# Key sums in one product of 384 rows, token factors spread by transfers, last columns in halves, and an opening by three queues, in a hybrid attention layer

## The chip, the core and the metric

The kernel runs on one core of a Trainium2 chip. The metric is the device time of one execution in microseconds. TensorE is called PE below (its weight loads PEld), VectorE DVE, ScalarE ACT, GpSimd POOL, and SyncE SP. SP, ACT and POOL can issue transfers; what each has issued stands in a queue of its own, and the 16 DMA engines serve all queues.

## What is computed

One layer of an encoder for 256 tokens (two blocks of 128) of width 2048, all in float32. It has two groups of eight heads of 128, then a feed-forward part with a causal convolution:

```python
h  = rms_norm(x)
p  = h @ w_in                      # q, k, v of both groups and the forget gates
a  = forgetting_attention(...)     # softmax with a bias of summed log forget gates
b  = stick_breaking_attention(...) # strictly causal, weights from suffix sums
x  = x + concat(rms_norm(a), rms_norm(b)) @ w_out
h  = rms_norm(x)
u  = causal_conv3(h @ w_up) + conv_b
x  = x + (silu(gate_of(u)) * value_of(u)) @ w_down        # d_ff = 5632

# stick breaking, one head
z             = q @ k.T * scale
log_beta      = log_sigmoid(z)
log_one_minus = where(mask, log_beta - z, 0)
suffix        = reversed_cumsum(log_one_minus, over keys) - log_one_minus
weights       = where(mask, exp(log_beta + suffix), 0)
out           = weights @ v
```

## The kernel before

**Products in three parts.** Weights arrive as float32 (`w_raw`, by SP's queue). ACT casts them to float32r (`w_hi`, L197), DVE subtracts that from the original (`w_lo`, L198), and activations are split in the same way. Each product is then the sum of three: high by high, low by high, high by low. Token-major results have 512 columns a product (`in_three`, L219), feature-major ones take 512 columns for both parts of hT by `w_hi` (L246) and 256 columns by `w_lo` (L253). A piece of weights is 1 MB in most stages.

**Order.** The opening and the feed-forward part have an order written out by hand for PE, DVE, ACT and SP (`manual_schedule`). Between them a scheduler orders the instructions of each engine. The feed-forward part is a list of steps: step n issues its loads six steps ahead, splits weights two steps ahead, and what follows a step (`follow`) runs in the steps after it. Within one engine, instructions run in their order, so a waiting instruction holds all behind it.

**Opening.** `opening` (from L353) computes the first 512 columns, the queries of the first four heads, while x is still arriving. `columns` (L125) turns the rows of the first norm's gains (`prow`) into a column `ga`, with the identity from the constants `cs`; `transposed_split` transposes x (L135), scales it by `ga` into the high part of hT on ACT (L140) and makes the low part on DVE (L143). `split_w` casts and splits weights (L374, L377), `multiply` (L386) accumulates. `keep_busy` (L349) sends products of a cleared tile `zeros` through PE while the first data are on their way. The weights of the first piece come as two blocks of 256 KB by ACT's queue; x, `cs` and the rest by SP's.

**Token factors.** The factor of RMSNorm for each token is not applied to x but to the results. `token_factors` computes it as a column per block (`rstd`, L114). Where results have tokens in partitions, it is used as it is. Where tokens run along the free axis (feature-major results), each partition needs all 256 factors in a row: `in_every_partition` multiplies a matrix of ones by two diagonal matrices `dg` (L163) on PE (L170) and copies the result from PSUM to a tile R (L171). R1 is used for the queries and keys of the stick-breaking heads (`R1q` at L558 is R1 times the scale), R2 in the feed-forward part (`convolved`, L695), from step 1 on.

**First heads.** `fox_rows` takes the query rows of four heads, forms the factor of each head's norm on DVE and ACT (L108 to L114), multiplies (`raw`, L313), and `to_heads` transposes on PE (L294).

**Stick breaking.** `sb_head` has the logits of a head in one PSUM tile `ps` of three blocks of 128 columns: `ps[:, 0]` for keys 0 to 127 by queries 0 to 127, `ps[:, 1]` for the same keys by queries 128 to 255, `ps[:, 2]` for keys and queries 128 to 255. `z0` is the first two, `z1` the third, `zz` all. The key sums are added to it by products with a triangle of -1 (`ntri[:, :P]`) and a square of -1 (`ntri[:, P:]`), once for each part of the split sums `sps` (L595 to L597).

**End.** `down_plain` computes the last rows of the down projection: for each 512 columns two pieces of weights of four row blocks. For the last 512 columns the second piece does token block 0 first and then token block 1; DVE adds each result to x (L792) and SP stores it (L794), for block 1 in two parts of 256 columns.

**POOL** issues the transfers of `c_rows` (L492, a row for each head written to DRAM) and `minus_c` (L493, the same rows read into all partitions), and some of the weights in the feed-forward part (L815).

Of the kernel before, what the change touches and what calls it, by code (L numbers as in the profile page):

```python
# [14 lines left out]
P = 128  # L15
# [26 lines left out]
def hybrid_layer(  # L42
# [123 lines left out]
    def in_every_partition(dg, n, pool):  # L166
        R = pool.tile([P, S], F32, name=f"R{n}")
        pr = psb.tile([P, S], F32, name="pr", tag="t")
        for t in range(NT):
            nc.tensor.matmul(pr[:, t * P : (t + 1) * P], ones, dg[t], start=t == 0, stop=t == NT - 1)  # L170
        dve.tensor_copy(R, pr)  # L171
        return R


# [99 lines left out]
    with ExitStack() as actx:  # L274
# [78 lines left out]
        def opening():  # L353

            acc = psa.tile([P, NT, 512], F32, name="acc", tag="acc")
            pairs = [[(0, 1), (1, 1)]] + [[(0, 2)]] * 7
            raws, parts = [], []

            def load_w(c, queue=nc.sync, which=(0, 1)):
                if c == len(raws):  # L360
                    raws.append(wraw.tile([P, 2048], F32, name="w_raw", tag="w_raw"))
                for i, n in pairs[c][which[0] : which[-1] + 1]:
                    queue.dma_start(
                        raws[c][:, i * 512 : (i + n) * 512].rearrange("p (a b) -> p a b", a=n),
                        rows_of(wi, 2 * c + i, n, 0, 512),
                    )
# [13 lines left out]

            def multiply(c, i, n, high):
                hi, lo = (p[:, i : i + n] for p in parts[c])
                order = [(j, l, hi) for j in range(n) for l in range(2)] if high else [(j, 0, lo) for j in range(n)]
                for m, (j, l, r) in enumerate(order):
                    for t in range(NT):
                        nc.tensor.matmul(  # L386
                            acc[:, t, :], of_half(hT[:, 2 * c + i + j], l, t), r[:, j, :],
                            start=high and c == i == m == 0, stop=not high and c == 7 and m == n - 1,
                        )
# [12 lines left out]
            columns(ga, prow[:KT, :], KT)  # L402
            keep_busy(0)
            split_w(0)
            keep_busy(6)

            def behind(c):
                transposed_split(2 * c + 2, ga)
                split_w(c + 1)

            for c in range(8):
                if 0 < c < 7:
                    behind(c)
                for i, n in pairs[c]:
                    if i == 0:
                        if c:
                            sums_of_squares(ss1, c // 2, [c % 2])
                        if c < 5:
                            if c % 2:
                                load_x(8 + 4 * (c // 2), 4)  # L420
                            load_w(c + 3)
                    for high in (True, False):
                        multiply(c, i, n, high)
                        if c == i == 0 and high:
                            behind(0)
                            sums_of_squares(ss1, 0, [0])
            return acc
# [7 lines left out]
        rstd1, dg1 = token_factors(ss1, 1)  # L435

        columns(pcol, prow, 50)
        masksR = at.tile([P, 4 * P], F32R, name="masksR")
# [28 lines left out]

        c_of = at.tile([P, NT, NH], F32, name="c_of")
        minus_c = at.tile([P, NH, S], F32, name="minus_c")
        dram = actx.enter_context(tc.tile_pool(name="dram", bufs=1, space=bass.MemoryType.DRAM))  # L470
        c_rows = dram.tile([NH, S], F32, name="c_rows")

        def gates():
# [79 lines left out]


        B0 = 3 * WF + NH
        R1 = in_every_partition(dg1, 1, at)
        R1q = at.tile([P, S], F32, name="R1q")
        dve.tensor_scalar(R1q, R1, QSCALE, None, op0=ALU.mult)  # L558

# [10 lines left out]
        def sb_head(h, qT, kT, v):  # L570
# [21 lines left out]

            for i in range(2):
                s = sps[:, i, :]
                mm(z0, ntri[:, :P], s[:, : 2 * P], start=False, stop=False, skip_group_check=True)  # L595
                mm(ps[:, 1, :], ntri[:, P:], s[:, 2 * P :], start=False, stop=False, skip_group_check=True)
                mm(z1, ntri[:, :P], s[:, 2 * P :], start=False, stop=i == 1, skip_group_check=True)  # L597
# [68 lines left out]
    tokens = []  # L666

    def parameters():
        pc = psb.tile([P, 4, NC2], F32, name="pcc", tag="t")
# [117 lines left out]
        yield  # L787

    def added(c, ps, t, op=ALU.add, final=False, n=512):
        for i in range(0, 512, n):  # L790
            xs = xt[t][:, c + i : c + i + n]
            dve.tensor_tensor(xs, xs, ps[:, i : i + n], op=op)  # L792
            if final:
                nc.sync.dma_start(of[t * P : (t + 1) * P, c + i : c + i + n], xs)  # L794
        yield

    def down_in_seven(part, c0):
# [70 lines left out]
    def down_plain(part, c):  # L868

        n = (part.f_hi - part.f_lo) // 4  # L870
        cell = []

        def piece(kh):
            mem = {}

            ends = c == D - 512 and kh == n - 1

            def loads():
                mem["raw"] = load(rows_of(wd, part.f_lo + 4 * kh, 4, c, 512))

            def prepare():
                mem["parts"] = split(mem["raw"], 4, 512)

            def matmuls():
                if kh == 0 and c == D - 512:
                    cell.extend(psf.tile([P, 512], F32, name="bank_a", tag="a") for _ in range(NT))
                elif kh == 0:
                    acc = psa.tile([P, NT, 512], F32, name="acc", tag="acc")
                    cell.extend(acc[:, t, :] for t in range(NT))
                for ts in [[t] for t in range(NT)] if ends else [range(NT)]:  # L890
                    in_three(
                        [cell[t] for t in ts], mem["parts"], 4,
                        lambda i, p, t: of_half(part.pairs[2 * kh + i // 2][:, :, i % 2], p, ts[t]),
                        kh == 0, kh == n - 1,
                    )
# [41 lines left out]
    for n in range(-LOAD, len(steps) + 8):  # L937
# [4 lines left out]
        with tc.high_priority(offset=2 * AHEAD) if n < 0 else nullcontext():  # L942
# [62 lines left out]
```

## Time and profile before

| | |
|---|---|
| median of three runs | 1116.93 us (1116.54 to 1117.72) |
| profiled execution | 1115.63 us |
| its span | 1113.7 us |
| PE busy | 1106.9 us, 99% |
| DVE busy | 862.7 us, 77% |
| ACT busy | 692.7 us, 62% |
| POOL busy | 27.2 us, 2% |
| read from memory over the span | 207 GB/s |

The profile is of one execution. A row of the timeline gives start, length, engine, line of the kernel, operation, output and inputs, and in brackets how long the engine was idle before and what ended that. PEq, SPq and the like are instruction queues. The chain of waits is followed back from the last instruction: at each step to what released it, or to the instruction before it on its engine; its rows are start, length and what, so that the length of a product there is its pace and not its way through the array.

### The profile page before, as it was taken

How to read it: one execution, taken by the hardware profiler on the slowest of the kernel's cores; microseconds unless marked ns; L12 is line 12 of the kernel's file. 1: busy time of each engine (PE TensorE's matmuls, PEld its weight loads, DVE VectorE, ACT ScalarE, POOL GpSimd, SP SyncE). 2: the span in 40 equal slices, each digit the busy share in tenths (PEclk: the TensorE clock that was granted, in tenths of full speed). 3: DMA queues.
4: the chain of work that ended last, by engine and by line, in shares of the span. 5: the costliest groups of instructions: out<-in, count | busy, mean ns of one | idle time of the engine just before them, and what ended most of it. 6: DMA issues, size and time to landing. Idle time of an engine off the chain costs nothing.

```text
span 1113.7 us, 14715 instructions
## 1 busy us (share of the span) xinstructions
PE 1106.9 (99%) x5873; PEld 957.9 (86%) x5873; DVE 862.7 (77%) x906; ACT 692.7 (62%) x849; POOL 27.2 (2%) x27
## 2 busy tenths in 40 slices
PE   9999999999999999999999999999999999999998
PEld 7998888888888888888888888888888888888886
DVE  5745666657666677788899898989989899989973
ACT  6544545355565567666777767775777667776751
POOL 0000000000000000000000000000000000000000
PEclk9999999999999999999999999999999999999999
DMA  8676656564445486496869696788859697697941
GB/s 260 213 227 227 190 152 189 155 185 153 152 152 164 137 271 207 126 263 181 259 211 254 208 265 218 227 243 228 248 184 251 219 266 248 193 266 195 297 161 67
DMA packets 172479, 231.34 MB, mean 208 GB/s; under 512 B 4192, under 2 KB 118266, under 8 KB 172282
## 3 DMA queue, kind: packets, MB, share of 16 engines
q1 hardware_dynamic: 162378, 209.93, 58.3%
q0 software_dynamic: 9712, 19.93, 10.2%
q8 instruction: 46, 0.75, 0.3%
q10 hardware_dynamic: 320, 0.53, 0.2%
q14 instruction: 23, 0.19, 0.0%
HBM read 228.28 MB, written 2.11 MB: 207 GB/s over the span
## 4 chain that ended last, share of the span: by engine, by line
PE 98%; DVE 1%; DMA 0%; ACT 0%; issue 0%; SPq 0%; DVEq 0%; ACTq 0%
PE pu L246 33%; PE acc L219 24%; PE pu L253 18%; PE bank_a L219 10%; PE bank_b L219 4%; PE bank_c L219 2%; PE acc L386 2%; PE ps_x L135 1%; DVE w_lo L198 1%; DMA cs<-in_cst_dram 0%; PE ps_z L576 0%; PE ps_o L604 0%; PE ps_s L506 0%; PE ps_o L536 0%; PE ps_h L294 0%; PE ps_p L530 0%
## 5 line engine op out<-in xcount | busy, mean ns | idle before, releaser
L198 DVE TENSOR_TENSOR w_lo<-w_raw,w_hi 128x2048 fp32r<-128x2048 f32 (+2 forms) x200 | 440.1, 2204 | 161.9 <-ACT w_hi L197 156.0
L197 ACT CAST w_hi<-w_raw 128x2048 fp32r<-128x2048 f32 (+2 forms) x200 | 368.1, 1841 | 239.4 <-PE acc L219 91.2
L246 PE MATMUL pu<-hT,w_hi 128*128 128x512 f32 x1664 | 397.6, 391 | 0.0
L246 PEld LDWEIGHTS pu<-hT,w_hi 128*128 128x128 f32 x1664 | 310.1, 188 | 63.2
L253 PEld LDWEIGHTS pu<-hT,w_lo 128*128 128x128 f32 x1664 | 213.6, 191 | 8.2
L253 PE MATMUL pu<-hT,w_lo 128*128 128x256 f32 x1664 | 216.2, 283 | 0.0
L219 PE MATMUL acc<-w_hi,hT 128*128 128x512 f32 (+1 forms) x576 | 126.0, 370 | 0.0
L219 PEld LDWEIGHTS acc<-w_hi,hT 128*128 128x128 f32 x576 | 101.6, 188 | 14.3
L709 ACT ACTIVATE tap<-up,ccol 128x256 f32<-128x256 f32 x176 | 74.6, 495 | 0.0
L198 DVE TENSOR_TENSOR w_lo<-w_sum,w_hi 128x2048 fp32r<-128x2048 f32 (+1 forms) x30 | 62.2, 2073 | 13.4 <-ACT w_hi L197 10.6
L197 ACT CAST w_hi<-w_sum 128x2048 fp32r<-128x2048 f32 (+1 forms) x30 | 51.9, 1731 | 22.8 <-PE pu L246 22.8
L219 PE MATMUL acc<-w_lo,hT 128*128 128x512 f32 (+1 forms) x288 | 64.6, 366 | 0.0
L219 PEld LDWEIGHTS acc<-w_lo,hT 128*128 128x128 f32 x288 | 51.6, 188 | 7.5
L219 PE MATMUL acc<-w_hi,oT 128*128 128x512 f32 x192 | 46.3, 393 | 0.0
L219 PE MATMUL bank_a<-w_hi,g 128*128 128x512 f32 x176 | 44.2, 392 | 0.0
L219 PEld LDWEIGHTS acc<-w_hi,oT 128*128 128x128 f32 x192 | 35.4, 188 | 7.0
L219 PEld LDWEIGHTS bank_a<-w_hi,g 128*128 128x128 f32 x176 | 31.8, 189 | 5.7
L219 PE MATMUL bank_a<-w_hi,s 128*128 128x512 f32 x144 | 36.5, 393 | 0.0
L219 PE MATMUL bank_b<-w_hi,s 128*128 128x512 f32 x144 | 36.4, 392 | 0.0
L714 DVE TENSOR_TENSOR gate<-gate,tap 128x512 f32<-128x512 f32 x44 | 30.3, 688 | 2.3
L714 DVE TENSOR_TENSOR val<-val,tap 128x512 f32<-128x512 f32 x44 | 30.3, 688 | 2.3
L815 POOL DMA_DIRECT2D w_raw<-in_w_down_dram x10 | 12.7, 1270 | 779.6 <-DVE s L761 373.9
(176 smaller groups left out, 1052.1 us busy)
## 6 DMA issues: line engine op xcount, KB each, us to landing
w_raw<-in_w_up_dram SPq DMA_DIRECT2D x88, 1024.0 KB, 5.8
w_raw<-in_w_down_dram SPq DMA_DIRECT2D x40, 1024.0 KB, 5.3
w_raw<-in_w_in_dram SPq DMA_DIRECT2D x36, 1024.0 KB, 5.3
w_raw<-in_w_out_dram SPq DMA_DIRECT2D x16, 1024.0 KB, 5.2
w_raw<-in_w_in_dram SPq DMA_DIRECT2D x12, 688.0 KB, 4.2
w_raw<-in_w_down_dram POOLq DMA_DIRECT2D x8, 1024.0 KB, 12.0
w_sum<-in_w_down_dram POOLq DMA_DIRECT2D x8, 1024.0 KB, 9.0
w_raw<-in_w_down_dram SPq DMA_DIRECT2D x8, 512.0 KB, 4.0
```

Source lines behind the costliest of these rows:

```text
L135: nc.tensor.transpose(ps[:, j, t * P : (t + 1) * P], xt[t][:, (k + j) * P : (k + j + 1) * P], ident)
L197: act.copy(hi[:, :n], raw[:, :n])
L198: dve.tensor_tensor(lo[:, :n], raw[:, :n], f32(hi[:, :n]), op=ALU.subtract)
L219: nc.tensor.matmul(o, lhs(i, l, t), r[:, i, :], start=starts and j == 0, stop=stops and j == 3 * n - 1, skip_group_check=more,)
L246: nc.tensor.matmul(acc[:, j, :], hi[:, i, j * P : (j + 1) * P], hT[:, k].rearrange("p a b -> p (a b)"), start=k == 0, stop=False,)
L253: nc.tensor.matmul(acc[:, j, S:], lo[:, i, j * P : (j + 1) * P], hT[:, k, 0, :], start=False, stop=k == KT - 1,)
L386: nc.tensor.matmul(acc[:, t, :], of_half(hT[:, 2 * c + i + j], l, t), r[:, j, :], start=high and c == i == m == 0, stop=not high and c == ...
L709: act.activation(taps[w][:, j, :], u[:, j, w : w + S], AF.Copy, scale=ccol[:, w, f : f + 1])
L714: dve.tensor_tensor(a, a, tap, op=ALU.add)
L815: nc.gpsimd.dma_start(mem[into][:, : nk * 512].rearrange("p (a b) -> p a b", a=nk), src, accum_op=ALU.add)
```

## The change

Five edits, in the order of the kernel:

- `token_factors` makes no diagonal matrices. `in_every_partition` writes each block's column of factors to a row in DRAM by POOL (128 elements of 4 bytes a transfer), and reads both rows into all partitions by a third transfer, which waits for the two. For R2 it is called right after the factors, and not in step 1 of the feed-forward part.
- The opening: `cs` and the rows of gains go to POOL's queue; the first 256 columns of x come as one transfer for each token block, on SP and on ACT; the first block of weights follows on SP, the second on ACT. DVE clears `zeros` and makes the first `w_hi`. PE gets 16 and 5 products of `keep_busy`, before 17 and 6.
- `sb_head`: one product of all 384 columns with the triangle, and one of 128 with the square.
- `added` has one part at each call.
- `down_plain`: for the last 512 columns token block 1 is computed as two results of 256 columns in tiles of their own. In the first piece the three results take turns, in the second they come one after the other, and each is added and stored when it is done.

In the built kernel `R1q` moves on DVE from 155 us, among the softmax work of the first group, to the place between L108 and L111 of the first query heads. Moved lines of the same text are left out here:

```diff
-        dg = []
         for t in range(NT):
-            dg.append(small.tile([P, P], F32, name="dg", tag="dg", bufs=2))
-            dve.tensor_scalar(dg[t], ident, rstd[:, t : t + 1], None, op0=ALU.mult)
-        return rstd, dg
...
-    def in_every_partition(dg, n, pool):
-        R = pool.tile([P, S], F32, name=f"R{n}")
-        pr = psb.tile([P, S], F32, name="pr", tag="t")
-        for t in range(NT):
-            nc.tensor.matmul(pr[:, t * P : (t + 1) * P], ones, dg[t], start=t == 0, stop=t == NT - 1)
-        dve.tensor_copy(R, pr)
+    def in_every_partition(rstd, n, pool):
+        row = dram.tile([NT, P], F32, name=f"row{n}")
+        R = pool.tile([P, S], F32, name=f"R{n}")
+        for t in range(NT):
+            nc.gpsimd.dma_start(row[t : t + 1, :].rearrange("t p -> p t"), rstd[:, t : t + 1])
+        nc.gpsimd.dma_start(R, row.rearrange("t p -> (t p)").unsqueeze(0).to_broadcast([P, S]))
         return R
...
-        nc.gpsimd.memset(zeros, 0.0)
+        dve.memset(zeros, 0.0)
...
-                    act.copy(hi[:, cols], raws[c][:, cols])
                     if c == i == 0:
+                        dve.tensor_copy(hi[:, cols], raws[c][:, cols])
                         transposed_split(0, ga)
+                    else:
+                        act.copy(hi[:, cols], raws[c][:, cols])
...
-            load_x(0, 2)
-            nc.sync.dma_start(cs[:, :P], cst[:, :P])
-            load_w(0, nc.scalar, [0])
-            nc.scalar.dma_start(prow[:KT, :], attn_norm[0].rearrange("(n p) -> n p", p=P))
+            nc.gpsimd.dma_start(cs[:, :P], cst[:, :P])
+            nc.gpsimd.dma_start(prow[:KT, :], attn_norm[0].rearrange("(n p) -> n p", p=P))
+            for t, queue in enumerate((nc.sync, nc.scalar)):
+                queue.dma_start(xt[t][:, : 2 * P], xf[t * P : (t + 1) * P, : 2 * P])
+            load_w(0, nc.sync, [0])
             load_w(0, nc.scalar, [1])
...
-            keep_busy(17)
+            keep_busy(16)
             columns(ga, prow[:KT, :], KT)
-            keep_busy(0)
             split_w(0)
-            keep_busy(6)
+            keep_busy(5)
...
-                mm(z0, ntri[:, :P], s[:, : 2 * P], start=False, stop=False, skip_group_check=True)
-                mm(ps[:, 1, :], ntri[:, P:], s[:, 2 * P :], start=False, stop=False, skip_group_check=True)
-                mm(z1, ntri[:, :P], s[:, 2 * P :], start=False, stop=i == 1, skip_group_check=True)
+                mm(zz, ntri[:, :P], s, start=False, stop=False, skip_group_check=True)
+                mm(ps[:, 1, :], ntri[:, P:], s[:, 2 * P :], start=False, stop=i == 1, skip_group_check=True)
...
-    rstd2, dg2 = token_factors(ss2, 2)
+    rstd2 = token_factors(ss2, 2)
+    tokens = [in_every_partition(rstd2, 2, const)]
...
     def down_plain(part, c):
...
+        ends = c == D - 512
+        sizes = [(0, 0, 512), (1, 0, 256), (1, 256, 256)] if ends else [(t, 0, 512) for t in range(NT)]
+        cells = []
...
+            def product(some):
+                hi, lo = mem["parts"]
+                order = [(i, l, hi) for i in range(4) for l in range(2)] + [(i, 0, lo) for i in range(4)]
+                for j, (i, l, r) in enumerate(order):
+                    g = part.pairs[2 * kh + i // 2][:, :, i % 2]
+                    for (t, c0, cols), o in some:
+                        nc.tensor.matmul(
+                            o, of_half(g, l, t), r[:, i, c0 : c0 + cols],
+                            start=kh == 0 and j == 0, stop=kh == n - 1 and j == 11,
+                        )
...
+                both = list(zip(sizes, cells))
+                for some in [[b] for b in both] if ends and kh == n - 1 else [both]:
+                    product(some)
...
             def follow():
-                for t in range(NT):
-                    yield from added(c, cell[t], t, final=True, n=256 if ends and t else 512)
+                for (t, c0, cols), o in zip(sizes, cells):
+                    yield from added(c + c0, o, t, final=True, n=cols)
...
-            if n == 1:
-                tokens.append(in_every_partition(dg2, 2, const))
```

More of the change, by code (lines that the diff above doesn't have):

```diff
@@ L159, in token_factors @@
         rsqrt(rstd, ssum, 1.0 / D, NT)
-        dg = []
-        for t in range(NT):
-            dg.append(small.tile([P, P], F32, name="dg", tag="dg", bufs=2))
-            dve.tensor_scalar(dg[t], ident, rstd[:, t : t + 1], None, op0=ALU.mult)
-        return rstd, dg
-    def in_every_partition(dg, n, pool):
-        R = pool.tile([P, S], F32, name=f"R{n}")
-        pr = psb.tile([P, S], F32, name="pr", tag="t")
-        for t in range(NT):
-            nc.tensor.matmul(pr[:, t * P : (t + 1) * P], ones, dg[t], start=t == 0, stop=t == NT - 1)
-        dve.tensor_copy(R, pr)
+        return rstd
+    dram = ctx.enter_context(tc.tile_pool(name="dram", bufs=1, space=bass.MemoryType.DRAM))
+    def in_every_partition(rstd, n, pool):
+        row = dram.tile([NT, P], F32, name=f"row{n}")
+        R = pool.tile([P, S], F32, name=f"R{n}")
+        for t in range(NT):
+            nc.gpsimd.dma_start(row[t : t + 1, :].rearrange("t p -> p t"), rstd[:, t : t + 1])
+        nc.gpsimd.dma_start(R, row.rearrange("t p -> (t p)").unsqueeze(0).to_broadcast([P, S]))
         return R
@@ L434, in hybrid_layer @@
         load_parameters(masks)
[L435 removed]
+        rstd1 = token_factors(ss1, 1)
         columns(pcol, prow, 50)
@@ L789, in added @@
     def added(c, ps, t, op=ALU.add, final=False, n=512):
[L790 to L794, printed above, removed]
+        xs = xt[t][:, c : c + n]
+        dve.tensor_tensor(xs, xs, ps, op=op)
+        if final:
+            nc.sync.dma_start(of[t * P : (t + 1) * P, c : c + n], xs)
         yield
@@ L882, in prepare @@
                 mem["parts"] = split(mem["raw"], 4, 512)
+            def product(some):
[8 more added lines that the diff above has]
+                        )
             def matmuls():
-                if kh == 0 and c == D - 512:
-                    cell.extend(psf.tile([P, 512], F32, name="bank_a", tag="a") for _ in range(NT))
+                if kh == 0 and ends:
+                    for i, (_, _, cols) in enumerate(sizes):
+                        pool, tag = (psf, "a") if i < 2 else (psb, "t")
+                        cells.append(pool.tile([P, 512], F32, name="bank_a", tag=tag)[:, :cols])
                 elif kh == 0:
                     acc = psa.tile([P, NT, 512], F32, name="acc", tag="acc")
[L889 to L895, printed above, removed]
+                    cells.extend(acc[:, t, :] for t in range(NT))
+                both = list(zip(sizes, cells))
+                for some in [[b] for b in both] if ends and kh == n - 1 else [both]:
+                    product(some)
             def follow():
-                for t in range(NT):
-                    yield from added(c, cell[t], t, final=True, n=256 if ends and t else 512)
+                for (t, c0, cols), o in zip(sizes, cells):
+                    yield from added(c + c0, o, t, final=True, n=cols)
             new_step(loads, None, prepare, matmuls, follow if kh == n - 1 else None)
```

6 lines of the change are left out of this document (1 added, 5 removed).

## The prediction

> **What bounds the kernel now.** I read the page first, then the chain of waits stretch by stretch, then the timeline at the places that the change touches.
>
> ```profile
> PE 1106.9 (99%) x5873; PEld 957.9 (86%) x5873; DVE 862.7 (77%) x906; ACT 692.7 (62%) x849; POOL 27.2 (2%) x27
> PE 98%; DVE 1%; DMA 0%; ACT 0%; issue 0%; SPq 0%; DVEq 0%; ACTq 0%
> ```
>
> TensorE (PE) is busy for 99% of the span and is 98% of the chain. So an instruction taken from PE is worth its whole pace, wherever its operands are ready, and a wait that reaches PE costs its whole length. GpSimd (POOL) is free, and PE stands still only in the first microseconds, after the token factors, and at the end. The change touches these three places, and two products in the middle. The profiled execution took 1115.63 us, its span is 1113.7 and 1.9 us lie around it. The sum below is made on the span and carried to the median of the runs, 1116.93, which is 1.3 us above the profiled one.
>
> **The opening.** Chain of waits, then the timeline's row of the first real weight load:
>
> ```profile
> 1.23 4.08 DMA cs<-in_cst_dram
> ...
> 7.69 0.73 PE acc L386 x2
> ...
> 10.79 0.44 PE ps_x L135 x4
> ```
> ```profile
> 5.42 0.13 PEld L125 LDWEIGHTS pp<-cs,prow 16*128 16x128 f32 x1 [1.25 <-DMA prow<-in_attn_norm_dram]
> ```
>
> Everything hangs on the identity (`cs`, 64 KB) and the norm rows (`prow`, 8 KB), which arrive together at 5.3 to 5.4 us, `cs` behind the first x on SP, `prow` behind the first weights on ACT. The DMA issues of the opening give their sizes (KB each, us to landing):
>
> ```profile
> w_raw<-in_w_in_dram ACTq DMA_DIRECT2D x2, 256.0 KB, 5.0
> x<-in_x_dram SPq DMA_DIRECT2D x2, 256.0 KB, 5.1
> ```
>
> The change gives `cs` and `prow` to POOL's queue, puts half of the first x at the head of SP and half at the head of ACT, the first weights second on SP, and moves the first `w_hi` copy to DVE, which is idle there until hT comes. What can it bring? A look at the DMA engines:
>
> ```profile
> 5.00:10.00 5.00, 4.40 (x25) 3.31 (x26) 2.48 (x6) 2.81 (x7) 0.00 (x0) 1.00 1.00 362
> ```
>
> Between 5 and 10 us they are full (share 1.00, 362 GB/s), and the bytes needed by the transposes at 10.79 stay the same. So beyond about 0.9 us an earlier start would only wait there for x: an estimate, the size of PE's idle time in these 5 us (5.00 less 4.40) and half as much again. That bounds the gain. On the other side, POOL issues `cs` first and `prow` after it, 0.6 to 0.7 us each (rows below), while SP and ACT issue both first weight blocks. If `prow` has to stand behind these, it comes after 832 KB (x, `cs`, two blocks) instead of 584 KB (x, `cs`, `prow`, one block), 248 KB later, at 362 GB/s 0.7 us; a little of that is saved in front of it. So the bounds are -0.9 and +0.6; I take -0.3, between them and nearer to the gain, since `cs` and x themselves stand behind less in either order. Two idle products fewer and the cleared tile on DVE cost nothing: PE waits for data behind both.
>
> **Token factors, what goes.** Chain of waits at the two places where the factors are spread by PE:
>
> ```profile
> 151.30 0.44 PE pr L170 x4
> ```
> ```profile
> 414.86 0.45 PE pr L170 x4
> ```
>
> Both stand on the chain with PE full on either side, so removing them gives -0.89. The DVE work that goes (`dg`, the copy of R) is off the path.
>
> **Token factors, what comes.** Each time POOL issues two column writes of 128 single elements and a read that waits for both and spreads them. What such a round trip costs is seen at `c_rows`, the one that exists: POOL's timeline, the issues with their time to landing, and the DMA queues from 95.2 to 98 and from 98.5 to 101:
>
> ```profile
> 92.53 0.69 POOL L492 DMA_DIRECT2D c_rows<-mine  x1 [91.49 <-ACT mine L491]
> 94.61 0.59 POOL L493 DMA_DIRECT2D minus_c<-c_rows  x1 [1.39 <-DMA c_rows<-mine]
> ```
> ```profile
> w_raw<-in_w_in_dram SPq DMA_DIRECT2D x12, 688.0 KB, 4.2
> ...
> minus_c<-c_rows POOLq DMA_DIRECT2D x1, 1024.0 KB, 7.0
> ...
> c_rows<-mine POOLq DMA_DIRECT2D x1, 8.0 KB, 1.8
> ```
> ```profile
> q1 hardware_dynamic: 417, 0.85, 93.4%
> ```
> ```profile
> q0 software_dynamic: 130, 0.97, 92.0%
> ```
>
> With the engines idle a write took 1.8 us and its reader could be issued 2.08 us after it. But the read, issued by 95.2, moved nothing until 98: SP's queue (q1) had the engines to itself, and only then did POOL's (q0) run, with 92%. So a small transfer of POOL stands behind the loads that SP has already issued. That decides when R1 and R2 come.
>
> The order of the built kernel puts `R1q` (which needs R1) on DVE right after `rs_a` of the first query heads, far earlier than today's 155 us. Timeline of DVE, then two loads of SP:
>
> ```profile
> 35.96 0.16 DVE L114 TENSOR_TENSOR rstd<-rs_y,rs_u 128x2 f32<-128x2 f32 x1
> ```
> ```profile
> 42.47 0.24 DVE L108 TENSOR_SCALAR rs_a<-ss 128x4 f32<-128x4 f32 x2
> 43.14 0.26 DVE L111 TENSOR_TENSOR rs_u<-rs_a,rs_y 128x4 f32<-128x4 f32 x2 [0.44 <-ACT rs_y L110]
> ```
> ```profile
> 38.68 0.37 SPq L190 DMA_DIRECT2D w_raw<-in_w_in_dram  x1
> ```
> ```profile
> 42.58 0.37 SPq L190 DMA_DIRECT2D w_raw<-in_w_in_dram  x1
> ```
>
> The factor is ready at 36.12. Two issues of about 0.69 and 2.08 us from the second one's start give landed columns at about 39.0, a little more for 256 tiny elements beside a load: 39.7. The read is issued by 40.4 and stands behind the load of 38.68, which lands 4.2 us after its issue, at 42.9; 128 KB more, 43.4. `R1q` (an estimate of 0.3 us, less than a pass over 256 columns of PSUM) ends at 43.7, where today `rs_u` starts at 43.14. Behind it in DVE's queue stand `rs_u`, `r` and `raw`; PE's head transposes wait for `raw`, so PE loses what DVE loses: +0.6. From below it is 0 (R1 in time), from above it is the third rival.
>
> For R2 the view is the same, with more cover:
>
> ```profile
> 418.81 0.69 DVE L695 TENSOR_TENSOR up<-t,R 128x512 f32<-128x512 f32 x1
> ```
> ```profile
> 429.31 0.69 DVE L693 TENSOR_TENSOR t<-pu,t 128x512 f32<-128x512 f32 x1
> ```
> ```profile
> 437.76 3.82 PE L246 MATMUL pu<-hT,w_hi 128*128 128x512 f32 x16
> ```
>
> This factor is ready at about 411 (the product that spreads it today stands at 414.86). The round trip without loads takes some 5 us (0.69 and 2.08 for the columns, about 2 for the read); a load of 1 MB in front of a step costs 2.8 us (95.2 to 98 above). With one or two in front of each of the two steps R2 comes at 421 to 427, 3 to 8 us after DVE wants it at 418.81. Queued behind that wait on DVE are `ccol`, two `w_lo` and the next `t`; on ACT the taps, the next cast and SiLU. But PE needs that `t` (it frees the PSUM bank) only at 437.76, and today it is done at 430.0. The cover is 7.8 us and some idle time on DVE and ACT more. So I put 0; beyond some 10 us of wait PE pays all the rest.
>
> **Key sums.** Chain of waits, one head of eight:
>
> ```profile
> 274.81 0.12 PE ps_z L595
> 274.93 0.06 PE ps_z L596
> 274.99 0.12 PE ps_z L597
> 275.11 0.17 PE ps_z L595
> 275.27 0.06 PE ps_z L596
> 275.33 0.11 PE ps_z L597
> ```
>
> Six products take 0.64 us. The columns do not get fewer (256+128+128 against 384+128); what goes are two starts. By the pace of the feature products (rows in the next fence: 3.65 us for 16 of 512, so 0.228 each) 384 columns take 0.171. The product of 128 columns behind it took 0.06 (L596) to 0.12 (L597); I take 0.11, as the next one has other weights, as after L597. Twice 0.28 is 0.56: 0.08 a head, -0.65 for eight. The bounds are -1.4 (0.06 each) and 0.
>
> **The end.** Chain of waits in the feed-forward part, then the timeline of the last additions and stores:
>
> ```profile
> 449.06 3.65 PE pu L246 x16
> 452.71 1.91 PE pu L253 x16
> ```
> ```profile
> 1109.59 0.75 DVE L792 TENSOR_TENSOR x<-x,bank_a 128x256 f32<-128x256 f32 x2 [2.03 <-PE bank_a L219]
> 1110.03 0.81 SPq L794 DMA_DIRECT2D out_dram<-x  x2
> ```
>
> In the last 512 columns the second row block's 24 products of 512 become 48 of 256: 24 x (2 x 0.119 - 0.228) = +0.26 on PE. Of the two additions and two stores behind the last product one each remains: the last store is issued about 0.43 earlier (half of 0.81 and the gap). Net -0.2, with one store in flight perhaps -0.4; +0.1 if the halves run slower.
>
> **The sum.** -0.3 - 0.89 + 0.6 + 0 - 0.65 - 0.2 = -1.44: the span goes to 1112.3, the profiled time to 1114.2, the median to 1115.5.
>
> **Rivals.** *Small transfers pass the loads.* If an engine alternates between queues, `prow` comes before the first weights (opening -0.9) and R1 by about 41.5 (no wait): -0.9 - 0.89 - 0.65 - 0.2 = -2.64, 1114.3. For it: in the opening the first transfers of SP and ACT land side by side (5.1 and 5.0 us after issue). Against it: 95.2 to 98 above. The Trainium skill, DMA: Bandwidth & Descriptors, section Queues, rings and completion order, says that each DMA engine serves its queue rows in turn, packet by packet; by that rule this rival is the forecast, but the trace disagrees where it shows POOL and SP together.
>
> *The change does not do what it says:* the product of 384 columns saves nothing and `prow` arrives late: +0.6 - 0.89 + 0.6 + 0 - 0.2 = +0.1, 1117.0. For it: columns bound a product, and no product of 384 columns is in this trace.
>
> *R1 falls behind one load more* (the other side). If the columns land later than about 42, the read stands behind the load issued at 42.58, which lands at 46.8; R1 at 47.3, `R1q` done at 47.6, 4.5 us on PE instead of 0.6: +2.4, 1119.4. The point is some 2 us of extra time in writing 256 single elements; nothing in the trace writes so small to DRAM. The same page, section Specifications, says that transfers under 512 B are read, modified and written; no row here shows its price.
>
> *R2 overruns its cover* by 2 us: +0.6, 1117.5.
>
> **How the numbers follow.** The forecast 0.45, small transfers pass 0.27, nothing saved 0.12, R1 a load later 0.10, R2 overruns 0.06. The forecast's own range is 1114.5 to 1116.6. The low end, 1113.4, is the passing case with the lower bound of the key sums (-0.9 - 0.89 - 1.4 - 0.3); the high end, 1117.8, takes in all cases but R1 a load later. 0.2%, about what a measurement of this kernel can tell from no change, is 2.2 us: faster means below 1114.7, most of the passing case (0.20) and the lower fifth of the forecast (0.09), 0.29; slower means above 1119.2, 0.08; the rest is 0.63.
>
> **What would show it.** In the changed profile: no `pr` product at 151 and 414; key sums of four products in about 0.56 us a head; `R1q` waiting for DMA R near 43 and PE's head transposes about 0.6 us later than their stage; DVE waiting several microseconds at L695 with PE still full; one addition of about 0.4 us behind the last product; the first products with hT near 7 us. Wrong would be a `pp` that moves by more than 1 us, an `R1q` wait over 2 us, or idle time of PE between 420 and 450.

## The result and the profile after

The changed kernel takes 1128.9 us (median; 1128.25 to 1130.42) against 1116.7 of the kernel before beside it: ratio 1.0119, 95% interval 1.0107 to 1.0131. It is 12 us slower. The profiled execution took 1128.59 us with a span of 1126.7, 13.0 us more than before.

The page of the changed kernel, its busy times and its chain by engine:

```profile
PE 1109.6 (98%) x5871; PEld 961.0 (85%) x5871; DVE 861.3 (76%) x902; ACT 691.7 (61%) x848; POOL 31.0 (3%) x34
PE 92%; DMA 4%; DVE 2%; ACT 1%; issue 1%; POOL 0%; ACTq 0%; POOLq 0%; DVEq 0%
```

PE fell from 98% of the chain to 92%, and 4% is now DMA. The view of DVE's waits names the places:

```profile
DVE up L694 <- DMA R<-row: 10.9, 1, 10.9
DVE R1q L558 <- DMA R<-row: 9.0, 1, 9.0
DVE ga L126 <- PE pp L125: 6.0, 1, 6.0
```

Where the 13.0 us arise is seen from the start of the same instruction in both timelines (us from the span's start):

| place | before | after | difference |
|---|---|---|---|
| norm transpose `pp` | 5.45 | 6.75 | +1.30 |
| parameter transposes, second `pp` | 30.17 | 33.13 | +2.96 |
| gate rows `pcr` | 91.43 | 105.02 | +13.59 |
| first feature products `pu` | 151.50 | 164.54 | +13.04 |
| last key sum `ps_z` | 344.22 | 356.68 | +12.46 |
| convolution parameters `pcc` | 420.71 | 432.73 | +12.02 |
| first down products `bank_a` | 465.59 | 478.98 | +13.39 |
| end of the last product | 1109.55 | 1123.02 | +13.47 |
| end of the span | 1113.65 | 1126.65 | +13.00 |

Three steps lose: the opening +2.96, R1 +10.63, R2 +1.37. Four win: R1's products -0.55, the stage with the key sums -0.58, R2's products -0.44, the end -0.39 (+0.08 and -0.47).

**The opening.** PE's timeline before (two rows) and of the changed kernel:

```profile
6.08 0.82 PE L349 MATMUL idle<-zeros 128*128 128x256 bf16 x6
6.80 1.61 PE L386 MATMUL acc<-w_hi,hT 128*128 128x512 f32 x4
```

```profile
6.75 0.25 PE L125 MATMUL pp<-cs,prow 16*128 16x16 f32 x1 [2.09 <-DMA prow<-in_attn_norm_dram]
6.93 1.11 PE L135 MATMUL ps_x<-cs,x 128*128 128x128 f32 x4
7.84 1.27 PE L348 MATMUL idle<-zeros 128*128 128x256 bf16 x5
8.76 2.06 PE L387 MATMUL acc<-w_hi,hT 128*128 128x512 f32 x4
```

The norm rows come 1.3 us later, and after a gap of 2.09 us everything on PE is slower for a while: the four products with hT take 2.06 us, 1.61 before, and five idle products 1.27, where six took 0.82. The granted clock does not show this: it reads 1.00 throughout the first 13 us in both profiles. PE starts at half pace in every profile here (idle products 0.21 us apart, later 0.11), and in that of the changed kernel it is still at half pace after the gap; more on that under e2.

**R1.** The chain of waits from the factor to the first head transposes and PE's row of these, then windows of before (two rows) and of the changed kernel (PE busy first, the granted clock PEclk and DMA share and GB/s last):

```profile
39.61 0.57 POOL row L169
40.18 8.18 DMA row<-rstd
...
48.91 5.96 DMA R<-row
54.87 0.02 issue
54.89 0.04 DVE R1q L558
...
56.73 1.09 PE ps_h L293 x4
```
```profile
56.73 1.09 PE L293 MATMUL ps_h<-cs,raw 128*128 128x128 f32 x4 [8.90 <-DVE raw L312]
```
```profile
42.00:48.00 6.00, 5.86 (x39) 5.61 (x38) 4.29 (x14) 2.76 (x7) 0.00 (x0) 1.00 0.47 139
48.00:54.00 6.00, 6.00 (x41) 5.98 (x40) 2.19 (x2) 3.99 (x5) 0.00 (x0) 1.00 0.69 213
```
```profile
42.00:48.00 6.00, 5.82 (x37) 5.54 (x36) 3.88 (x7) 3.23 (x6) 0.00 (x0) 1.00 0.72 32
48.00:54.00 6.00, 0.00 (x0) 0.00 (x0) 0.00 (x0) 0.00 (x0) 0.54 (x1) 0.67 0.72 227
54.00:58.00 4.00, 1.27 (x6) 1.31 (x7) 3.11 (x12) 0.15 (x1) 0.00 (x0) 0.50 0.01 3
58.00:64.00 6.00, 6.00 (x34) 5.99 (x33) 1.90 (x2) 3.13 (x5) 0.00 (x0) 0.81 0.36 117
```

The second column write needs 8.18 us after its issue and the read 5.96. From 42 to 48 us the DMA engines are busy for 0.72 of the time and move 32 GB/s; nearly all of that share (71.7%) is packets of SP's loads, which hardly get on. PE stands still for 8.90 us, and when work comes back its granted clock is 0.50, then 0.81. By windows of 1 us the half clock lasts from 50.1 to 60.3 us, so PE works some 3.6 us at half pace, which loses 1.8 (an estimate from these times). With the 8.90 that makes about R1's 10.63, more than DVE's wait of 9.0.

**R2.** The chain at the second factor:

```profile
423.57 12.28 DMA row<-rstd
...
436.41 5.68 DMA R<-row
...
450.29 0.70 DVE t L692
450.99 0.04 issue
451.04 3.92 PE pu L245 x16
```

Columns 12.28 us, read 5.68, a wait of 10.9 us at L694, and PE stands still at 451.04 for 1.10 us, because `t` behind it on DVE frees the bank late.

**Key sums and end.** The chain of one head after, with the products behind it, and of the last addition:

```profile
295.33 0.18 PE ps_z L595
295.51 0.06 PE ps_z L596
295.56 0.23 PE ps_z L595
295.79 0.06 PE ps_z L596
295.85 5.57 PE acc L218 x24
```
```profile
1117.43 5.60 PE bank_a L889 x36
1123.03 0.02 issue
1123.06 0.42 DVE x L790
```

Four products take 0.52 us instead of 0.64. The 24 products behind them take 5.57 us where 5.49 to 5.51 was usual before, so a part of that comes back. Between the first and the last `ps_z` the stage is 0.68 us shorter (75.80 to 75.12), 0.08 to 0.09 a head.

### The profile page after: what moved, and what is told of

It reads as the page before. It is cut to its first block, busy times and chain, and to the rows that moved or that the text cites. A ratio compares the mean times of both kernels' runs of the same rounds, so it can differ in the third digit from the quotient of the medians.

```text
span 1126.7 us, 14715 instructions
## 1 busy us (share of the span) xinstructions
PE 1109.6 (98%) x5871; PEld 961.0 (85%) x5871; DVE 861.3 (76%) x902; ACT 691.7 (61%) x848; POOL 31.0 (3%) x34
## 4 chain that ended last, share of the span: by engine, by line
PE 92%; DMA 4%; DVE 2%; ACT 1%; issue 1%; POOL 0%; ACTq 0%; POOLq 0%; DVEq 0%
PE pu L245 31%; PE acc L218 20%; PE pu L252 16%; PE bank_a L218 9%; PE bank_b L218 4%; PE acc L889 3%; PE bank_c L218 2%; PE acc L387 2%; DMA row<-rstd 2%; DMA R<-row 1%; PE bank_a L889 1%; DVE w_lo L197 1%; ACT w_hi L196 1%; PE ps_x L135 1%; DMA w_raw<-in_w_up_dram 0%
## 5 line engine op out<-in xcount | busy, mean ns | idle before, releaser
L694 DVE TENSOR_TENSOR up<-t,R 128x512 f32<-128x512 f32 x44 | 30.4, 692 | 12.4 <-DMA R<-row 10.9
L218 PE MATMUL bank_a<-w_hi,g 128*128 128x512 f32 x144 | 36.4, 392 | 0.0
L701 ACT ACTIVATE gate<-up,ccol 128x256 f32<-128x256 f32 x44 | 24.0, 594 | 19.4 <-DVE ccol L671 10.4
## 6 DMA issues: line engine op xcount, KB each, us to landing
w_raw<-in_w_down_dram POOLq DMA_DIRECT2D x8, 1024.0 KB, 12.3
```

What stands on the lines that cost most here:

```text
L218: nc.tensor.matmul(o, lhs(i, l, t), r[:, i, :], start=starts and j == 0, stop=stops and j == 3 * n - 1, skip_group_check=more,)
L694: dve.tensor_tensor(u[:, :, 2:], t2, R, op=ALU.mult)
L701: act.activation(a[:, j, :], u[:, j, 2:], AF.Identity, scale=ccol[:, 2, f : f + 1], bias=ccol[:, 3, f : f + 1],)
```

## The experiments

Each was timed in rounds beside the kernel before on the same chip, which took 1115.6 to 1115.8 us there, a microsecond less than above. The ratios below are to that neighbour. The runs come from three chips (e1 to e4, e5 to e8, e9 to e12).

**Factors by products again, new opening** (`e1`), and **key sums and halves alone** (`e3`):

```diff
 e1, against the changed kernel
-    nc.gpsimd.dma_start(row[t : t + 1, :].rearrange("t p -> p t"), rstd[:, t : t + 1])
-    nc.gpsimd.dma_start(R, row ... to_broadcast([P, S]))
+    nc.tensor.matmul(pr[:, t * P : (t + 1) * P], ones, dg[t], ...)
+    dve.tensor_copy(R, pr)
 e3, against the kernel before: only the product over zz and the new added() and down_plain()
```

> The changed kernel with the token factors spread by two products of TensorE again, as before the change; opening, key sums and last columns stay changed. Theory: the transfers of the two factors cost most. From the two traces: R1 costs 13.59 - 2.96 = 10.6 us (gate products 91.59 to 105.18, second transpose of parameters 30.24 to 33.20), R2 about 1.5, less 0.89 for the two products that they replace. So this kernel is 1128.9 - 10.6 - 1.5 + 0.9 = 1117.7, range 1117 to 1118.5. Rival, the opening's delay is the main cause and drags the loads behind it: then the time stays above 1124.

> The kernel before with two parts of the change: key sums by one product of 384 columns, last columns in two halves. From the traces: 0.64 to 0.52 us a head, eight heads, -0.96; the end, products ending at 1109.56 of 1113.7 before and 1123.03 of 1126.7 after, 4.14 against 3.67, -0.47, less 0.16 for halves (5.44 to 5.60). Sum -1.3: 1115.5. Rival: the sums' gain is lost to other work of the head, then 1116.4.

Measured: e1 1117.28 (ratio 1.0011, 1.0002 to 1.0020), e3 1114.42 (0.9986, 0.9976 to 0.9995). The transfers of the factors are the 11 to 12 us. e1 and e3 differ by the opening alone: 2.9 us. Key sums and halves together bring 1.3.

**Old opening, all else changed** (`e2`: queues, idle products, copy and cleared tile as before).

> The changed kernel with the opening of before (x, identity, weights and norm rows on SP and ACT, zeros cleared by POOL, first w_hi on ACT, 17, 0 and 6 idle products). Theory: the opening's 3.0 us (parameter transposes 30.24 before, 33.20 after) are lost for good, so 1128.9 - 3.0 = 1125.9. Rival: the factor's way through DRAM sets the end of that stage whatever the opening does, so an earlier start is eaten by a longer wait for R1: 1128 to 1129.

Measured: 1128.35 (1.0111, 1.0095 to 1.0126), so the rival holds: the opening's gain does not arrive. The traces show where it goes. The second `pp` starts at 31.24 instead of 33.13, `pcr` at 104.11 instead of 105.02, `bank_a` at 478.99, level with the changed kernel's 478.98. (Its opening itself ends 1.07 us behind that of the kernel before. PE is longer at its starting pace there: the six idle products behind the norm transpose take 1.49 us, 0.82 before. The same opening passes to full pace at 3.8 us in the profile before, at 4.8 in e10, at 6.9 in e9 and at 9.4 in e2, by the traces' record of the clock, so this part differs from execution to execution.) Of the 1.9 us half is lost behind R1, where PE's 23 products after the gap take longer (first line e2, second the changed kernel, chain of waits): the half clock ends at 60.6 us in e2 and at 60.3 in the changed kernel, although PE resumes 1.75 us earlier in e2. The rest is lost at R2, where DVE's wait grows from 10.9 to 11.8:

```profile
56.06 5.71 PE acc L218 x23
```
```profile
57.81 4.82 PE acc L218 x23
```

**R1 used late** (`e4`): the changed kernel, but the constant goes into the heads' own operation.

```diff
-        R1q = at.tile([P, S], F32, name="R1q")
-        dve.tensor_scalar(R1q, R1, QSCALE, None, op0=ALU.mult)
-    dve.tensor_tensor(dst[...], t2, scale ..., op=ALU.mult)
+    dve.scalar_tensor_tensor(dst[...], t2, scale, R1 ..., op0=ALU.mult, op1=ALU.mult)
```

> The changed kernel without R1q: the query heads multiply by the constant and by R1 in one DVE operation, so DVE's first use of R1 comes after 150 us instead of near 43 us. The transfers stay as they are. Theory: the 10.6 us are DVE's queue standing behind the wait for R1, so with the first use late they vanish: 1128.9 - 10.6 = 1118.3. Rival, the tiny writes clog the DMA engines (32 GB/s at a share of 0.72 from 42 to 48 us) and the weights come late whatever DVE does: a load issued at 41.87 landed at 52.08, 10.2 us; then PE still loses 4 us or more there: 1122 to 1126.

Measured: 1118.16 (1.0020, 1.0011 to 1.0030; single executions from 1116.8 to 1120.7), 10.7 us less than the changed kernel. The transfers and their clog are still there, but PE does not feel them. Windows of e4:

```profile
42.00:48.00 6.00, 5.86 (x40) 5.61 (x39) 5.56 (x17) 3.23 (x6) 0.00 (x0) 1.00 0.78 32
48.00:54.00 6.00, 6.00 (x41) 5.98 (x41) 2.77 (x2) 3.49 (x5) 0.54 (x1) 1.00 0.95 322
```

So the loss is DVE's queue, standing behind one small multiplication that nobody needs for another 100 us. That the weights come late (32 GB/s here too) did not matter.

**Two long rows instead of 256 elements** (`e5`). Its kernel leaves out the turning of columns into rows, so its R does not hold the tokens' own factors; only its time counts.

```diff
-        for t in range(NT):
-            nc.gpsimd.dma_start(row[t : t + 1, :].rearrange("t p -> p t"), rstd[:, t : t + 1])
+        two = const.tile([NT, P], F32, name=f"two{n}")
+        dve.tensor_copy(two, rstd[:NT, 0:1].to_broadcast([NT, P]))
+        nc.gpsimd.dma_start(row, two)
```

> The changed kernel, but the 256 single elements that POOL writes for each factor become one write of two rows of 512 B; DVE fills the two rows from the factor of one token (left out: the turning of columns into rows, so the factors in R are not the tokens' own). Issue places, the read and R1q's place on DVE stay. Theory: the single elements hold the DMA engines (32 GB/s at a share of 0.72 from 42 to 48 us, landings spread from 42.4 to 48.4), so with two long rows the write lands about 2 us after its issue, the read goes at about 42.3 instead of 48.9, R1 is there at 46 to 47 (behind the load issued at 41.87) and DVE waits 1 to 3 us instead of 9.0; R2's wait shrinks under its cover. 1128.9 - 7 - 1.5 = 1120.4, range 1118.5 to 1122.5. Rival, the writes of POOL wait behind SP's loads whatever their form: they land 6 us or more after the issue again and the time stays above 1126.

Measured: 1119.46 (1.0027, 1.0016 to 1.0038). Its chain and its waits:

```profile
39.16 3.34 DMA row<-two
...
42.79 4.40 DMA R<-row
```
```profile
DVE up L695 <- DMA R<-row: 5.6, 1, 5.6
DVE R1q L559 <- DMA R<-row: 2.0, 1, 2.0
```

The form of the write is what made it late: 3.34 us instead of 8.18 at R1. At R2 the same two rows took 6.9 us, 12.28 before them, so the form is about half of it there. R2's wait of 5.6 us costs PE nothing (from `pcc` to `bank_a` 44.88 us, as before). R1's wait of 2.0 still costs 3.5 us (second `pp` to `pcr` 64.77 us against 61.26 before, and 61.04 in e1). The windows show why:

```profile
48.00:52.00 4.00, 2.95 (x12) 2.98 (x13) 3.01 (x6) 0.69 (x1) 0.00 (x0) 0.66 0.13 47
52.00:56.00 4.00, 4.00 (x26) 3.98 (x26) 0.99 (x1) 2.37 (x4) 0.00 (x0) 0.91 0.57 176
```

A gap of 1.9 us on PE is followed by clocks of 0.66 and 0.91; by windows of 1 us the half clock lasts from 49.3 to 52.7. This does not come every time: two of the seven executions took 1117.3 us with a mean clock of 1.000 over the span, the other five 1118.5 to 1120.7 with 0.997 or 0.998.

**The write by its form** (`e8`, `e12`): chains of writes on POOL in the kernel before, each followed by a read of 1 KB that waits for it, beside SP's loads.

```diff
 e8
+   for _ in range(6):
+       nc.gpsimd.dma_start(probe[0:1, :].rearrange("t p -> p t"), rstd1[:, 0:1]);  read
+       nc.gpsimd.dma_start(probe.rearrange("t p -> p t"), rstd1);                  read
+       nc.gpsimd.dma_start(probe, ident[0:2, :]);                                  read
 e12, five times, each followed by a read
+       wide[0:1, 0:32] <- rstd1[0:32, 0:1]      # 32 neighbours        read L562
+       wide[:, 0:1]    <- rstd1[:, 0:1]         # 128, 512 B apart     read L564
+       wide[0:2] as 128 pairs <- rstd1          # 128 pairs            read L566
+       wide            <- ident                 # 128 rows of 512 B    read L568
+       wide[0:1, :]    <- rstd1[:, 0:1]         # 128 neighbours       read L560
```

> The kernel before with a chain of probes on POOL's queue after c_rows: six times, one after the other, a write of 128 single elements (one column of the factor), of 256 single elements in one transfer (both columns), and of two rows of 512 B, each followed by a read of the 1 KB, which waits for it; nothing uses them. They measure the write by its form beside the weight loads of SP. Theory: 128 elements take about 4 us to land, 256 about 8, two long rows about 2. Rival: all three take the same and it varies with the loads under way.

> The kernel before with another chain of probes on POOL's queue, five times over: writes of 32 single elements next to each other, of 128 single elements 512 B apart, of 128 pairs (8 B) next to each other, of 128 rows of 512 B, and of 128 single elements next to each other, each followed by a read of 1 KB that waits for it. Theory: what is slow is many small writes into the same rows of DRAM, so 128 elements 512 B apart and 128 rows take 2 to 4 us, 128 neighbours 9, 128 pairs 9, 32 neighbours 4. Rival: the number of descriptors counts and not where they go: all with 128 take about 9, the rows of 512 B too. Second rival: the size of a piece counts, then elements 512 B apart take 9 too, and only the rows of 512 B are fast.

Waits of POOL's reads (total, times, longest), e8 then e12:

```profile
POOL back L562 <- DMA probe<-rstd: 54.8, 6, 10.4
POOL back L560 <- DMA probe<-rstd: 52.4, 6, 9.9
...
POOL back L564 <- DMA probe<-cs: 17.6, 6, 4.0
```
```profile
POOL back L560 <- DMA wide<-rstd: 34.9, 4, 9.4
POOL back L566 <- DMA wide<-rstd: 24.1, 5, 5.2
POOL back L562 <- DMA wide<-rstd: 22.7, 5, 5.5
...
POOL back L564 <- DMA wide<-rstd: 16.4, 5, 4.5
POOL back L568 <- DMA wide<-cs: 16.0, 5, 4.4
```

A mean wait is total by times. In e8: 128 neighbouring elements 8.7 us, 256 in two rows at once 9.1 (not twice as much, against the theory), two long rows 2.9. In e12: 128 neighbours 8.7, 128 pairs 4.8 (9 was expected), 32 neighbours 4.5, 128 elements 512 B apart 3.3, 128 rows of 512 B 3.2. So neither the number of pieces nor their size alone makes the write slow: 128 single elements are as quick as 128 rows when they lie 512 B apart. It is small pieces side by side. From 3.3 to 8.7 us for 128 and to 4.5 for 32 gives some 0.04 us for each single neighbour, as an estimate; the 256 elements and the pairs cost less a piece. Counted by pieces in one row of 512 B, 128 take 8.7 and 9.1 us, 64 (the pairs) 4.8, 32 take 4.5 and one 3.3. The order fits a cost of pieces in the same row, the sizes only roughly, and no run varies that alone. The time of both kernels (1115.11 and 1115.63 in one execution each) does not show the probes.

**The opening** (`e6`, `e7`, both to be compared with e1's 1117.28 and 1.0011).

```diff
 e6
-            keep_busy(16)
+            keep_busy(28)
 e7
-            nc.gpsimd.dma_start(cs[:, :P], cst[:, :P])
-            nc.gpsimd.dma_start(prow[:KT, :], attn_norm[0].rearrange("(n p) -> n p", p=P))
+            nc.sync.dma_start(cs[:, :P], cst[:, :P])
+            nc.scalar.dma_start(prow[:KT, :], attn_norm[0].rearrange("(n p) -> n p", p=P))
```

> The kernel with factors by products, new opening, key sums and halves (1117.28 us), with 28 idle products in front of the norm transpose instead of 16, so that TensorE has no gap until the norm rows are there. Against the kernel with the old opening (1114.42) the new one costs 2.9 us: the norm transpose is 1.83 us later (7.05 against 5.22), and after the gap of 2.4 us the granted clock is 0.75 from 7 to 9 us and 0.60 from 9 to 12. Theory: the gap brings the lower clock, so filling it gives back the other 1.1: 1116.2. Rival: the low clock there comes with the start whatever PE does before: 1117.3.

> The same kernel (1117.28 us) with the identity issued first on SP and the norm rows first on ACT, instead of both on POOL; all the rest of the new opening stays. Theory: POOL's place is the cause (issues end at 1.99 and 2.53, the norm rows land at 6.9 in that trace behind the first weights on two queues), so identity and norm rows land by about 4, the first weights 0.2 later, and the opening is as fast as the old one or 0.5 faster: 1113.9 to 1114.5. Rival: half a first x on either queue or the weights of SP are the cause: above 1116.

Measured: e6 1116.66 (1.0007, 0.9998 to 1.0016), e7 1114.42 (0.9986, 0.9977 to 0.9996). The first line is e1's window after the gap, the second e6's, where there is none:

```profile
7.00:9.00 2.00, 1.95 (x12) 1.56 (x12) 0.76 (x3) 1.13 (x3) 0.00 (x0) 0.75 1.03 391
```
```profile
7.00:9.00 2.00, 1.91 (x12) 1.15 (x11) 0.97 (x4) 1.33 (x3) 0.00 (x0) 1.00 1.04 392
```

With idle products up to the norm rows the clock stays at 1.00, and `pcr` starts at 93.11 instead of 93.95, 0.84 us earlier; the medians differ by 0.6 and the ratios by 0.4 us, which the intervals tell neither from 0 nor from the expected 1.1. With `cs` and `prow` at the head of SP and ACT the whole loss is gone: POOL's place was the cause. But e7 only equals e3, with `pp` at 4.58 against 5.22: being earlier there buys nothing, since `pcr` starts at 91.48 in e7 and 91.12 in e3.

**Versions that keep the idea** (`e9`, `e10`, with the old opening), and **the key sums alone** (`e11`).

```diff
 e10, against e3
-    four products of ones by dg, at both places
+    nc.tensor.transpose(pr[:NT, :P], rstd, ident)
+    dve.tensor_copy(two, pr[:NT, :P])
+    nc.gpsimd.dma_start(row, two)
+    nc.gpsimd.dma_start(R, row ... to_broadcast([P, S]))
-        R1q = ...            (e9 too; e9 has the change's element writes, for R1 only)
```

In both the constant goes into the heads' own operation, as in e4.

> The kernel with old opening, key sums and halves (1114.42 us), and of the token factors only R1 by the transfers of the change, with single elements, and without R1q (the constant goes into the heads' own operation). R2 stays with the products. Theory: the slow landing is harmless where the first use is 100 us away, so only the 0.44 us of R1's products goes: 1114.0, range 1113.7 to 1114.3. Rival: the slow weight loads from 42 to 52 us reach TensorE without the opening's 3 us of distance: 1115 or more.

> As e9, but for both factors TensorE turns the two columns into two rows by one transpose (in place of four products), DVE copies them, and POOL writes two rows of 512 B; R1 is asked for before the query heads, R2 at the place of today's products. Theory: each transpose takes about 0.1 us against 0.44, R2 comes about 10 us after its transpose, within the cover of about 10 us: 1114.42 - 0.7 = 1113.7. Rival: R2 asked for at 414 instead of 411 comes too late, TensorE loses 1 to 2 us near 437: 1114.7 to 1115.7.

> The kernel before with the key sums by one product of 384 columns alone. From the two traces 0.64 to 0.52 us a head: -0.96, against the 0.65 that the prediction had; 1114.8, if the halves bring the other 0.3 to 0.4 of the 1.33 of both. Rival: the halves bring more than the sums, then above 1115.1.

Measured: e9 1114.05 (0.9985, 0.9976 to 0.9993), e10 1113.79 (0.9986, 0.9977 to 0.9995), e11 1115.05 (0.9994, 0.9985 to 1.0003). e10 beats both kernels; that it beats e9 or e3 is within the intervals. Its trace shows what was meant, the chain at the second factor and DVE's wait:

```profile
413.52 0.11 PE pr L168
413.63 3.64 PE pu L247 x16
```
```profile
DVE up L693 <- DMA R<-row: 7.4, 1, 7.4
```

The transpose takes 0.11 us instead of 0.45, and 7.4 us of wait on DVE still lie under the cover (`pcc` to `bank_a` 44.88 us). e11 alone is not told from no change; its trace has the 0.68 us (`ps_z` 268.12 to 343.24, 75.12 us).

## Why the prediction was wrong, step by step

It said 1115.5, with no measurable change as the likeliest. Its sum was -1.44, the trace has +13.0. All three signs that it had named for being wrong are there: `pp` moved by 1.30 us, `R1q` waits 9.0, and PE stands still before 451 us.

- **The round trip of R1 failed first, at its price for the columns.** It took 1.8 us of `c_rows` (8 rows of 1 KB) and "a little more for 256 tiny elements". The elements took 8.18, and e5 and e8 show that the form does that. The read behind them took 5.96 where 3.0 was allowed (40.4 to 43.4), so R1 was there at 54.87 and not at 43.4. This was the point that the third rival had named (some 2 us of extra time in writing); it got a chance of 0.10 because nothing in the trace before wrote so small.
- **The rival's own price was too small as well**: +4.5 us on PE, against 10.63. It stopped at the next load's landing (`R1q` done at 47.6) and did not add that the element writes delay the loads too (12 loads of 688 KB took 4.2 us in the page before, 7.2 after), nor that PE comes back from a gap with half its clock. The factor itself was also 3.2 us later (39.31 instead of 36.12), for the opening.
- **The place of the wait was right.** `R1q` stood behind `rs_a`, and DVE's queue behind it; e4 takes it away and with it the loss. Here the prediction accepted an avoidable wait: R1's first real use is after 150 us.
- **R2**: the cover was about right (5.6 and 7.4 us cost nothing in e5 and e10, 10.9 costs 1.37), its landing was not: `up` started at 442.19, 18.9 us after the factor was ready (423.28), where 10 to 16 were allowed. Again the columns, 12.28 us.
- **The opening** (-0.3, bounds -0.9 and +0.6) came out at +2.96. It weighed that `prow` might stand behind both first weight blocks (+0.7); it lands 1.3 us later. It gave no price at all to PE standing idle until then, the 0.84 us between e1 and e6. "Two idle products fewer cost nothing" was not tried by itself; e6, with twelve more, shows that idle products up to the data's arrival keep PE at full clock.
- **Right**: R's products (-0.89, measured -0.99 with their surroundings), the key sums (-0.65, measured -0.68; the products went from 0.64 to 0.52, a larger gain than the predicted 0.56, and the following products gave part of it back, so that the two numbers lie so close is in part luck), the end (-0.2, measured -0.39), and the sign of each.
- **Small transfers pass the loads** was the prediction's second case. The Trainium skill, DMA: Bandwidth & Descriptors, Queues, rings and completion order, says that each DMA engine serves its queues in turn. Here R's read, issued at 48.91, landed at 54.87 and the load of SP issued at 45.76 at 55.13, side by side; in e5 the load issued at 41.19 landed at 45.49 and the read issued at 42.79 only at 47.19. These rows do not settle the rule, and neither case had the slow columns that decided.

On the clock: the Trainium skill, TensorE: Matmul & The Clock Gate, Part 1: The HAM clock gate, gives half rate after an idle window of about 3.4 us. The 0.50 after PE's 8.9 us agrees. The gaps of 1.9 us (e5) and 2.4 us (e1) each brought a half clock for 3.4 us (49.3 to 52.7 and 8.0 to 11.4), so here a shorter gap was enough; the gap of 1.10 us at R2 left the clock at 1.00. On small writes: the Trainium skill, DMA: Bandwidth & Descriptors, Specifications, says that under 512 B data are read, modified and written. The traces agree that side by side they are slow, but 128 elements 512 B apart took the time of full rows, so the size alone does not decide; why neighbours are slow, the runs do not show.

## What to carry to other kernels

A wait is priced by what stands behind it in the waiting engine's queue: before a transfer replaces a computation, its first consumer has to move to where the value is really needed, and then even a slow transfer costs nothing that the medians show (e4 at R1, e9). A gap on a busy TensorE costs its length and can cost some microseconds at half clock after it, so a wait there is to be counted at more than its length. Filler products up to the moment when data arrive kept the clock up in e6, though the gain of 0.6 us is within the intervals. To turn a column into a row, a write of whole rows landed in 3.3 and 6.9 us (e5), behind one small transpose in 5.0 and 5.7 (e10), and single elements side by side in 8.2 and 12.3 (the changed kernel).

## What was not expected of the hardware

- Writing 128 neighbouring elements of 4 B to DRAM took 8.7 us to land, 32 neighbours 4.5, 128 elements 512 B apart 3.3, 128 rows of 512 B 3.2.
- While such writes are under way, SP's loads hardly move: 32 GB/s from 42 to 48 us at a DMA share of 0.72 (0.78 in e4), against 228 GB/s at 0.77 in e5 with long rows. Beside the probes of e8 the 1 MB loads took 9.8 us (median, 98 to 300 us), 5.4 without them.
- After a gap of 1.9 to 2.4 us PE's granted clock was 0.66 to 0.75 in e5 and e1, after 8.9 us 0.50; the two short gaps cost 3.5 us in all (e5) and some 0.8 us beyond the wait (e1 against e6).
- The stretches of full and half clock between the first rise and the last are whole multiples of 3.41 us: 3.41 at half (e1, e4, e5), 10.24 at half (the changed kernel, e2), 37.55 at full (the changed kernel, e5). That the clock is decided on such a grid is inferred from these lengths. It would explain why e5's executions differ.
- At the start PE runs at half pace and passes to full between 3.8 us (before) and 12.5 us (the changed kernel). The view of the granted clock reads 1.00 until its first record, so there the pace of the products is the sign to read.
